# A hybrid S5 / SSD / gated-DeltaNet trunk: side tasks cut into smaller pieces, the residual's scale and bias applied in the output projection, and two merge gates computed earlier

## Chip, cores and metric

One Trainium2 chip, one of its cores. The metric is the device time of one execution in microseconds (us), the median of several runs; lower is better.

## What is computed

Two decoder layers (DEPTH = 2) over 528 tokens (16 meta tokens and 512 of input), width 1024, everything in float32. An input LayerNorm makes `h`; each layer then does

```python
proj = h @ w_in[layer]
y_a = _s5_branch(...)      # diagonal complex state space, 48 groups, then gelu and a half-GLU
y_b = _ssd_branch(...)     # Mamba-2 style chunked scan, SiLU gate, RMSNorm
y_c = _gdn_branch(...)     # gated DeltaNet, 6 heads, chunked, RMSNorm, SiLU gate
branches = jnp.stack([y_a, y_b, y_c], axis=2)
outs = jnp.einsum('btnw,nwd->btnd', branches, w_branch[layer])
gates = jax.nn.sigmoid(gate_logits.reshape(bsz, t, N_BRANCH, D_MODEL) + b_gate[layer])
merged = jnp.sum(gates * outs, axis=2)
h = _layer_norm(ALPHA * h + merged @ w_out[layer], ln_g[layer], ln_b[layer])
```

and the meta tokens are dropped at the end. `_layer_norm` is `(z - mean) * rsqrt(var + eps) * g + b`.

## The kernel before

**Main stream and tasks.** The kernel writes its instructions in one pass of a Python program, and each engine runs its own instructions in the order in which they were written. The main stream is a list of items (`layer_items`, line 1704). Most are `Gemm` (line 570): 128 output channels over all tokens, the weights in pairs of 128x128 tiles, one pair being a "sub". For each sub ScalarE rounds the raw weight `wr` to `wh`, and VectorE (sometimes GpSimd) makes the rest `wl = wr - wh` (`Sub.prep`, line 509); TensorE then multiplies `wh` by the high part of the activations, `wh` by their low part, and `wl` by their high part: 12 matmuls of 264 columns for a sub. At most four subs are prepared ahead (`NSUB`), and four raw weight loads of two subs each (`NRAW`).

Everything else (convolution tails, the scalars of the heads, the gated-DeltaNet, SSD and S5 branches, norms) is a task: a Python generator that gives way at each `yield`. After each step of a Gemm, `pump` (line 458) lets tasks run that are due by a clock that the program keeps of its own writing. A plain `yield` makes a task due when what it just wrote is thought to end, `yield LEAD` 1.5 us before that. All that a task writes between two yields stands in one run in the queues of its engines, and the next split `wl` stands behind it.

**Names that matter here.** `head_scalars` (line 691) makes per-head scalars on tiles `sc`, `sc_p`, `sc_g`; `conv` (665) adds three taps to a channel tile (`q`, `k`, `v`, `x` or `bc` from `craw`); `rsqrt` (363) is eleven short VectorE instructions; `s5_params` (1268) makes the S5 tables on `s5t`, `s5f` through `together` (1256), which gave way after ten steps. `s5_task` (1545) runs one half of the S5 groups: `s5_mats` makes `Z`, `T` and `V` for four groups (T goes through DRAM: three writes `dK<-Kt`, eight reads `s5t<-dK`), `s5_core` multiplies `V` with the input `ub` (eight loads `ub<-dus`), scans, and multiplies again into `Y`, which ScalarE copies to `ys`. When a half is done, `ys` goes to DRAM (`dys<-ys`), and `s5_gelu` reads it back as `yc` and makes the rows `vhi`, `vlo` that the GLU's Gemms read. The loads all stand in one queue, that of SyncE (SP), in the order in which they were written.

**The layer's end.** In `merge_all` (1815) each branch n and each eighth d of the width has a gate Gemm and an output Gemm. Some gates (`KEPT`, line 52) are computed early, at places where the main stream has no other work, written to DRAM (`dgate`) and read back (`Back`) when they are due. The order is: branch 2, four kept gates, branch 1, wait for task `v` (the gelu rows), six GLU Gemms, six `za` Gemms, branch 0, and `OutProj` (1883) in four quarters of 256 columns, chunk of tokens by chunk.

**The residual.** LayerNorm leaves `z` normalised but without `g` and `b` (those reach the transposed `hTh`, `hTl` in `to_channels`, 393). A task `keep_task` (1686), due when all five token tiles are normalised, multiplies each by `g` and adds `b` with two instructions of 1024 columns (`ln_affine`, 388) and writes the tile to `hdram`, from where `o_pre` (1871) loads it as `zt` for the output projection.

Of the kernel before, what the change touches and what calls it, by code (L numbers as in the profile page):

```python
# [17 lines left out]
P = 128  # L18
D = 1024
# [32 lines left out]
KEPT = [(0, d) for d in range(2, 8)] + [(1, 6), (1, 7)]  # L52
# [187 lines left out]
def hybrid_trunk(ctx: ExitStack, tc: tile.TileContext, A: dict, out: bass.AP):  # L240
# [122 lines left out]
    def rsqrt(dst, x, shape, tag):  # L363
# [23 lines left out]

    def ln_affine(z, n, gb, bb):
        tte(z[:n], z[:n], gb[:n], MUL)
        yield LEAD  # L390
        tte(z[:n], z[:n], bb[:n], ADD)
# [273 lines left out]
    def conv(l, ci, ps, dst, bias):  # L665
# [8 lines left out]
        yield  # L674
# [16 lines left out]
    def head_scalars(l, smT, hs):  # L691
# [23 lines left out]
        V.reciprocal(out=s, in_=s)  # L715
        tt(V, s, s, e, MUL)
# [95 lines left out]
    def gdn_task(l, grp, hs, st):  # L812
# [26 lines left out]
        rsqrt(r, x, sh, "g_r")  # L839
# [256 lines left out]
        rsqrt(f, m, h3, "go_f")  # L1096
# [123 lines left out]
    def ssd_post(l, hs, st, to):  # L1220
# [12 lines left out]
        rsqrt(r, m, [P, NC], "sn_r")  # L1233
# [22 lines left out]
    def together(*chains):  # L1256

        chains, n = list(chains), 0
        while chains:
# [4 lines left out]
            if n >= 10:  # L1264
# [3 lines left out]
    def s5_params(l):  # L1268
# [124 lines left out]
        for k in (1, 2, 4):  # L1393
# [4 lines left out]
            tt(V, t[1], xi, yi, MUL)  # L1398
            tt(V, t[2], xr, yi, MUL)
# [56 lines left out]
    def s5_mats(l, hf, qd, q, b, out):  # L1456
# [88 lines left out]
    def s5_task(l, hf, st):  # L1545
# [3 lines left out]
        nxt = {}  # L1549
        yield from s5_mats(l, hf, 0, s5q, w["b"], nxt)  # L1550
# [120 lines left out]

    class Do:
# [7 lines left out]
    def ln_task(l, z, t0, n, st):  # L1680

        yield from ln_norm(z, n, st)
        yield
        yield from to_channels(z, t0, n, l)

    def keep_task(l, zs, gb, bb):

        for z, t0, n in zs:
            yield from ln_affine(z, n, gb, bb)
            yield  # L1690
            DMA.dma_start(out=hdram[l][t0:t0 + n, :], in_=z[:n])
# [471 lines left out]
```

## Time and profile before

| what | value |
|---|---|
| median of 3 runs (lowest to highest) | 1737.22 us (1730.16 to 1737.72) |
| the profiled execution, its own time | 1739.94 us |
| its span, first to last instruction | 1738.2 us |
| mean granted clock of TensorE | 0.972 of full speed |
| TensorE (PE) matmuls, busy | 1627.3 us, 94% |
| VectorE (DVE), busy | 1317.2 us, 76% |
| ScalarE (ACT), busy | 824.4 us, 47% |
| GpSimd (POOL), busy | 173.4 us, 10% |

In the rows below, a group of instructions reads `out<-in` by the program's names, with the shape, the number of them and their time. `[7.06 <-DVE wl]` is idle time of the engine ahead of the instruction and what ended it. Nearly all instructions carry line 229, a helper's, so names tell them apart. `PEclk` is the clock granted to TensorE as a share of full speed.

### The profile page before, as it was taken

To read this page: it belongs to the slowest core of one execution; us is meant where nothing else is said; L and a number is where in the kernel's file an instruction comes from. 1 tells how busy PE (TensorE), PEld (TensorE's weight loads), DVE (VectorE), ACT (ScalarE), POOL (GpSimd) and SP (SyncE) were. 2 spreads that over 40 slices of the span, in tenths; PEclk is the share of its full clock that TensorE was granted. 3 is DMA by queue.
4 is the path that set the end of the run, shared out by engine and by line. 5 is a ranking of instruction groups with operands and counts; after the bars stand their busy time and mean duration, and the time that the engine had idled before them with its cause. 6 is when DMAs were issued, how large, how long until landed. Compare 5 with 4: busy or idle time off the path is not lost.

```text
span 1738.2 us, 40832 instructions
## 1 busy us (share of the span) xinstructions
PE 1627.3 (94%) x15583; PEld 1554.7 (89%) x15583; DVE 1317.2 (76%) x3399; ACT 824.4 (47%) x2059; POOL 173.4 (10%) x314
## 2 busy tenths in 40 slices
PE   6799899989999899999989998999899989999997
PEld 5789899988899899999979998898888988999997
DVE  7987869778967876685678687697799869765665
ACT  5356554335673334434254655453366533453432
POOL 5000000110001000100130000101100001000013
PEclk9899999989999999999999999999999999999998
DMA  5223321343234444334423233223431452533352
GB/s 162 92 80 84 97 69 56 102 75 88 58 76 113 91 120 129 97 94 136 138 75 117 81 94 90 56 62 92 87 89 51 105 106 84 140 121 113 115 186 82
DMA packets 160147, 169.71 MB, mean 98 GB/s; under 512 B 67344, under 2 KB 98192, under 8 KB 159952
## 3 DMA queue, kind: packets, MB, share of 16 engines
q1 hardware_dynamic: 159952, 167.10, 34.8%
q8 instruction: 123, 2.02, 0.5%
q14 instruction: 72, 0.59, 0.1%
HBM read 144.40 MB, written 22.64 MB: 96 GB/s over the span
## 4 chain that ended last, share of the span: by engine, by line
PE 68%; DVE 16%; DMA 6%; issue 3%; ACT 3%; SPq 2%; POOL 1%; DVEq 0%; POOLq 0%; ACTq 0%
PE pj L229 49%; PE wo L229 5%; DVE wl L229 3%; SPq L229 2%; DMA wr<-in_w_main_dram 2%; PE y L229 2%; PE Y L229 2%; DMA dU<-UL 1%; PE seg L229 1%; DVE s5t L229 1%; DVE pr L229 1%; DVE s5w L229 1%; PE o L229 1%; PE z L229 1%; DVE UL L229 1%
## 5 line engine op out<-in xcount | busy, mean ns | idle before, releaser
L229 PE MATMUL pj<-hTh,wl 128*128 128x264 f32 (+1 forms) x2432 | 504.0, 288 | 35.1 <-DVE wl L229 34.9
L229 PE MATMUL pj<-hTh,wh 128*128 128x264 f32 (+1 forms) x2432 | 525.8, 297 | 1.5 <-ACT wh L229 1.5
L229 PE MATMUL pj<-hTl,wh 128*128 128x264 f32 (+1 forms) x2432 | 502.5, 287 | 0.0
L229 ACT ACTIVATE wh<-wr 128x256 fp32r<-128x256 f32 x820 | 327.2, 413 | 275.1 <-PE pj L229 227.7
L229 DVE TENSOR_TENSOR wl<-wr,wh 128x256 fp32r<-128x256 f32 x743 | 301.2, 429 | 163.6 <-ACT wh L229 160.8
L229 PEld LDWEIGHTS pj<-hTh,wl 128*128 128x128 f32 x2432 | 385.0, 193 | 41.0 <-DVE wl L229 40.7
L229 PEld LDWEIGHTS pj<-hTh,wh 128*128 128x128 f32 x2432 | 383.2, 193 | 9.5 <-issue 4.3
L229 PEld LDWEIGHTS pj<-hTl,wh 128*128 128x128 f32 x2432 | 385.8, 192 | 0.0
L229 POOL TENSOR_TENSOR wl<-wr,wh 128x256 fp32r<-128x256 f32 x77 | 64.9, 843 | 908.0 <-ACT wh L229 847.5
L229 PE MATMUL pj<-yhi,wh 128*128 128x264 f32 (+1 forms) x576 | 118.0, 286 | 2.0 <-ACT yhi L229 1.0
L229 PE MATMUL pj<-ylo,wh 128*128 128x264 f32 (+1 forms) x576 | 116.0, 283 | 0.5 <-DVE ylo L229 0.5
L229 PE MATMUL pj<-yhi,wl 128*128 128x264 f32 (+1 forms) x576 | 115.8, 282 | 0.0
L229 PEld LDWEIGHTS pj<-yhi,wh 128*128 128x128 f32 x576 | 88.5, 188 | 3.7 <-ACT yhi L229 1.4
L229 PEld LDWEIGHTS pj<-ylo,wh 128*128 128x128 f32 x576 | 88.6, 188 | 0.9 <-DVE ylo L229 0.9
L229 PEld LDWEIGHTS pj<-yhi,wl 128*128 128x128 f32 x576 | 88.7, 188 | 0.2 <-DVE wl L229 0.2
L229 ACT ACTIVATE segr<-triu,sc_glo 128x128 fp32r<-128x128 f32 (+1 forms) x168 | 52.3, 375 | 1.0 <-PE sS L229 1.0
L229 ACT ACTIVATE segr<-triu,sc_ghi 128x128 fp32r<-128x128 f32 (+1 forms) x168 | 52.3, 375 | 0.4 <-DVE x L229 0.2
L229 ACT ACTIVATE craw<-pj 128x528 f32<-128x528 f32 x56 | 34.0, 608 | 37.6 <-PE pj L229 37.5
L229 PE MATMUL wo<-wo,mhi 128*128 128x256 f32 x256 | 47.4, 283 | 0.2 <-DVE zt L229 0.2
L229 ACT ACTIVATE gth<-pj,pars 128x528 f32<-128x528 f32 (+1 forms) x48 | 33.1, 690 | 29.3 <-PE pj L229 29.3
L229 DVE TENSOR_TENSOR s5w<-s5w,s5w 128x132 f32<-128x132 f32 (+1 forms) x144 | 40.8, 297 | 3.0
L229 DVE TENSOR_TENSOR s5w<-V,tab 128x264 f32<-128x264 f32 x48 | 18.5, 427 | 32.2 <-PE V L229 32.2
(387 smaller groups left out, 2801.7 us busy)
## 6 DMA issues: line engine op xcount, KB each, us to landing
wr<-in_w_main_dram SPq DMA_DIRECT2D x304, 256.0 KB
wr<-in_w_branch_dram SPq DMA_DIRECT2D x48, 256.0 KB
wr<-in_w_out_dram SPq DMA_DIRECT2D x32, 256.0 KB
s5t<-dK SPq DMA_DIRECT2D x192, 32.0 KB
wr<-in_w_branch_dram SPq DMA_DIRECT2D x48, 128.0 KB
zt<-hdram SPq DMA_DIRECT2D x8, 512.0 KB
dus<-us SPq DMA_DIRECT2D x12, 264.0 KB
ub<-dus SPq DMA_DIRECT2D x32, 99.0 KB
```

Source lines behind the costliest of these rows:

```text
L229: r = f(*args, **kw)
```

## The change

It has four parts.

1. **Smaller pieces.** `yield LEAD` is added inside `rsqrt` (after each of three rounds), between the taps of `conv`, in `head_scalars`, in the S5 mats and tables; `together` gives way after six steps in place of ten; `s5_task` gives way after every part of a core or of the mats, where it ran one part of each.
2. **`ub` first.** `s5_task` writes the eight `ub` loads ahead of the first `s5_mats`, where they stood behind it.
3. **Residual.** `keep_task` and `ln_affine` go. The normalised tile is written to `hdram` at once, ahead of the transposes, and `OutProj` multiplies by `g` and adds `b` on each chunk's 256 columns ahead of the chunk's products. `g` and `b` of a layer are loaded with the first two `zt` tiles, into slots of the tag `bc`.
4. **Gates, and what the SSD norm waits for.** The last two kept gates are (0, 0) and (0, 1) in place of (1, 6) and (1, 7). So branch 1 computes its gates 6 and 7 in place, ahead of the wait for `v`, and branch 0 reads all eight back. `ssd_post` waits for the mark `xc` (branch 2 merged) where it waited for the second S5 half `fB`.

```diff
-KEPT = [(0, d) for d in range(2, 8)] + [(1, 6), (1, 7)]
+KEPT = [(0, d) for d in range(2, 8)] + [(0, 0), (0, 1)]
...
             stt(dst, t, 1.5, dst, ADD, MUL)
+            yield LEAD
...
         for i in range(3):
             fma(dst, raw[:, i:i + T], w[:, i:i + 1], dst)
-        yield
+            yield LEAD if i < 2 else None
...
         V.reciprocal(out=s, in_=s)
+        yield LEAD
...
             stt(p, p, 1.0 / d, s2, ADD, MUL)
+            if d in (13, 7):
+                yield LEAD
         stt(p, p, 1.0, s, ADD, MUL)
+        yield LEAD
...
-        while f"fB{l}" not in done:
+        while f"xc{l}" not in done:
             yield WAIT
...
-            if n >= 10:
+            if n >= 6:
...
         tte(z, bc(b["c"][:, gl], 2, 9), bc(q["pr"][:, gg], 3, 16), MUL)
+        yield LEAD
         tte(u, bc(b["cx"][:, gl], 2, 9), bc(q["pi"][:, gg], 3, 16), MUL)
+        yield LEAD
...
-        nxt = {}
-        yield from s5_mats(l, hf, 0, s5q, w["b"], nxt)
         while "us" not in st:
             yield WAIT
...
             DMA.dma_start(out=ub[16 * j:16 * j + 16], in_=src[:, :, NB8 * j:NB8 * j + NB8])
+        nxt = {}
+        yield from s5_mats(l, hf, 0, s5q, w["b"], nxt)
...
-                    if next(t, "end") == "end":
+                    r = next(t, "end")
+                    if r == "end":
                         live.remove(t)
-                if live:
-                    yield
+                    else:
+                        yield r
...
         yield from ln_norm(z, n, st)
         yield
+        keep(l, z, t0, n)
         yield from to_channels(z, t0, n, l)
-    def keep_task(l, zs, gb, bb):
...
+    def keep(l, z, t0, n):
+        DMA.dma_start(out=hdram[l][t0:t0 + n, :], in_=z[:n])
...
+                    zh = zt[c][:n, 256 * qn:256 * qn + 256]
+                    for x, op in zip(zt["in"], (MUL, ADD)):
+                        tte(zh, zh, x[:n, 256 * qn:256 * qn + 256], op)
                     if n < 32:
                         few_products(c)
```

**VectorE, layer 0, the head scalars beside the first convolutions.** `sc` and `sc_p` belong to `head_scalars`, `q` to a convolution, `s5t` to the S5 tables, `wl` are the weight splits that TensorE needs. Before:

```order
75 L229 TENSOR_SCALAR sc_576<-sc_576 128x90
76 L229 RECIPROCAL sc_576<-sc_576 128x90
77 L229 TENSOR_TENSOR sc_576<-sc_576 128x90 x2
78 L229 TENSOR_SCALAR sc_p_658<-sc_576 128x90
79 L229 SCALAR_TENSOR_TENSOR sc_p_658<-sc_p_658,sc_576 128x90 x8
80 L229 TENSOR_SCALAR sc_576<-sc_576 128x90
81 L229 SCALAR_TENSOR_TENSOR sc_576<-sc_p_658,sc_576 128x90
82 L229 TENSOR_TENSOR sc_g_670<-sc_576,pars 128x90
83 L229 TENSOR_SCALAR sc_g_670<-sc_g_670,m_107 128x18
84 L229 CAST sc_ghi_673<-sc_g_670 128x90
85 L229 SCALAR_TENSOR_TENSOR q_588<-craw_589,pars,q_588 128x528 x3
86 L229 TENSOR_TENSOR wl_685<-wr_502,wh_684 128x256
```

Now:

```order
65 L229 SCALAR_TENSOR_TENSOR q_578<-craw_579,pars,q_578 128x528
66 L229 TENSOR_TENSOR sc_566<-sc_566 128x90 x2
67 L229 TENSOR_SCALAR sc_p_625<-sc_566 128x90
68 L229 SCALAR_TENSOR_TENSOR sc_p_625<-sc_p_625,sc_566 128x90 x2
69 L229 TENSOR_TENSOR wl_636<-wr_444,wh_635 128x256
70 L229 SCALAR_TENSOR_TENSOR s5t_513<-s5t_513 128x48 x6
71 L229 SCALAR_TENSOR_TENSOR q_578<-craw_579,pars,q_578 128x528
72 L229 TENSOR_TENSOR wl_661<-wr_495,wh_660 128x256
73 L229 SCALAR_TENSOR_TENSOR sc_p_625<-sc_p_625,sc_566 128x90 x3
74 L229 TENSOR_TENSOR wl_685<-wr_495,wh_684 128x256
```

Between two splits there stood 21 instructions of the scalars and the convolution; now three splits stand among them.

**SyncE's queue, layer 0, the start of the second S5 half.** `wr` are raw weights, `dK` and `s5t` the way of T through DRAM, `ub` the S5 input. Before:

```order
204 L229 DMA dK<-Kt_8068 16x128
205 L229 DMA dK<-Kt_8068 32x128
206 L229 DMA dK<-Kt_8068 16x128
207 L229 DMA s5t_8076<-dK 16x4x128 x8
208 L229 DMA wr_8095<-in_w_main_dram 128x512
209 L229 DMA wr_8141<-in_w_main_dram 128x512
210 L229 DMA ub_8155<-dus_4413 16x24x66 x8
```

Now:

```order
202 L229 DMA ub_8111<-dus_4394 16x24x66 x8
203 L229 DMA wr_8134<-in_w_main_dram 128x512
204 L229 DMA wr_8174<-in_w_main_dram 128x512
205 L229 DMA wr_8213<-in_w_main_dram 128x512
206 L229 DMA dK<-Kt_8232 16x128
207 L229 DMA dK<-Kt_8232 32x128
208 L229 DMA dK<-Kt_8232 16x128
209 L229 DMA s5t_8240<-dK 16x4x128 x8
```

The eight `ub` loads now stand ahead of the eleven transfers of T, and T's come last.

**SyncE's queue, layer 1, the end of the second S5 half.** `dys` is the S5 output on its way to DRAM, `yc` its way back, `dgate` a kept gate. Before:

```order
599 L229 DMA dys_21715<-ys_20412 16x24x66 x8
600 L229 DMA dgate_88<-gth_21730 128x512
601 L229 DMA wr_21738<-in_w_main_dram 128x512
602 L229 DMA wr_21775<-in_w_branch_dram 128x512
603 L229 DMA dgate_88<-gth_21808 128x512
604 L229 DMA wr_21816<-in_w_branch_dram 128x256
605 L229 DMA wr_21855<-in_w_main_dram 128x512
606 L229 DMA wr_21895<-in_w_main_dram 128x512
607 L229 DMA wr_21932<-in_w_branch_dram 128x512
608 L229 DMA wr_21950<-in_w_branch_dram 128x256
609 L229 DMA yc_21961<-dys_19584 128x3x528
```

Now:

```order
610 L229 DMA dys_22179<-ys_20668 16x24x66 x8
611 L229 DMA yc_22189<-dys_19897 128x3x528
612 L229 DMA wr_22203<-in_w_branch_dram 128x512
613 L229 DMA wr_22221<-in_w_branch_dram 128x256
614 L229 DMA wr_22258<-in_w_main_dram 128x512
```

The read back of the first half now stands directly behind the writes of the second.

## Rows read from the trace of the kernel before

**Rows 1.** Page, part 1: busy time, share of the span, instructions.

```profile
PE 1627.3 (94%) x15583; PEld 1554.7 (89%) x15583; DVE 1317.2 (76%) x3399; ACT 824.4 (47%) x2059; POOL 173.4 (10%) x314
```

**Rows 2.** Chain that ended last, its longest piece: start, length, instructions.

```profile
759.90 77.15 PE pj L229 x632
```

**Rows 3.** Waits of PE: who for whom, us in total, times, longest.

```profile
PE pj L229 <- DVE wl L229: 35.4, 27, 7.1
PE V L229 <- DMA wr<-in_w_main_dram: 11.2, 3, 3.9
...
PE fb L229 <- DVE q L229: 3.0, 1, 3.0
...
PE V L229 <- DMA ub<-dus: 2.0, 1, 2.0
```

**Rows 4.** Timeline near 60 us, DVE and PE: start, length, instruction, idle before.

```profile
59.20 2.27 DVE L229 SCALAR_TENSOR_TENSOR sc_p<-sc_p,sc 128x90 f32<-128x90 f32 x8
...
62.58 2.37 DVE L229 SCALAR_TENSOR_TENSOR q<-craw,pars,q 128x528 f32<-128x528 f32 x3
...
65.34 0.81 PE L229 MATMUL pj<-hTh,wl 128*128 128x264 f32 x2 [7.06 <-DVE wl L229]
```

**Rows 5.** Stretches of 20 us: busy PE, PEld, DVE, ACT, POOL; granted clock; DMA; GB/s.

```profile
60.00:80.00 20.00, 14.66 (x92) 14.30 (x93) 19.27 (x75) 6.28 (x16) 0.20 (x2) 0.74 0.14 44
400.00:420.00 20.00, 17.85 (x166) 15.58 (x166) 14.35 (x50) 10.24 (x38) 1.20 (x1) 0.83 0.29 87
...
860.00:880.00 20.00, 20.00 (x177) 19.24 (x177) 12.65 (x33) 5.60 (x16) 2.98 (x4) 1.00 0.25 83
...
920.00:940.00 20.00, 16.56 (x112) 15.99 (x111) 17.32 (x44) 7.02 (x20) 0.20 (x2) 0.83 0.36 117
1240.00:1260.00 20.00, 15.28 (x185) 14.32 (x184) 12.17 (x45) 6.12 (x14) 2.05 (x5) 0.83 0.44 92
```

**Rows 6.** Tile `xin`, layer 0's residual: ns of one (min/median/max), first and last start.

```profile
L229 DVE TENSOR_TENSOR xin<-xin,ln_in_g x5: 1205/1214/1881, 32.4 to 55.0; 128x1024 f32<-128x1024 f32 x4, 16x1024 f32<-16x1024 f32 x1
```

**Rows 7.** The loads of `ub`: SyncE's timeline, and a piece of the chain.

```profile
557.36 1.94 SPq L229 DMA_DIRECT2D s5t<-dK  x1
...
560.29 4.15 SPq L229 DMA_DIRECT2D ub<-dus  x8
...
371.65 7.24 DMA ub<-dus
```

**Rows 8.** Groups of instructions by form: busy us, ns of one, idle before.

```profile
L229 DVE TENSOR_TENSOR wl<-wr,wh 128x256 fp32r<-128x256 f32 x743 | 301.2, 429 | 163.6 <-ACT wh L229 160.8 <-PE pj L229 1.0
...
L229 DVE BATCH_NORM_STATS2 lnst<-zt 128x6 f32<-128x256 f32 x32 | 13.7, 428 | 1.1
L229 DVE SCALAR_TENSOR_TENSOR zt<-zt,wo 128x256 f32<-128x256 f32 x32 | 13.4, 417 | 22.7 <-PE wo L229 20.5 <-DMA zt<-hdram 2.1
...
L229 POOL TENSOR_TENSOR wl<-wr,wh 128x256 fp32r<-128x256 f32 x77 | 64.9, 843 | 908.0 <-ACT wh L229 847.5 <-DMA dys<-ys 19.9 <-DVE vlo L229 19.8
```

**Rows 9.** Timeline near 39 us: a POOL instruction and a split on DVE beside it.

```profile
39.15 3.92 POOL L229 TENSOR_SCALAR_AFFINE_SELECT sel<-ones 18x768 bf16<-18x768 bf16 x3
39.40 1.11 DVE L229 TENSOR_TENSOR wl<-wr,wh 128x256 fp32r<-128x256 f32 x1
```

**Rows 10.** Timeline at the end of the second S5 half, layer 0, then layer 1.

```profile
649.04 0.39 ACT L229 ACTIVATE ys<-Y 128x264 f32<-128x264 f32 x1 [1.56 <-PE Y L229]
...
666.31 0.65 ACT L229 ACTIVATE gl<-yc 128x528 f32<-128x528 f32 x1 [1.10 <-DMA yc<-dys]
...
1498.84 0.39 ACT L229 ACTIVATE ys<-Y 128x264 f32<-128x264 f32 x1 [2.32 <-PE Y L229]
...
1524.00 0.65 ACT L229 ACTIVATE gl<-yc 128x528 f32<-128x528 f32 x1 [3.31 <-DMA wr<-in_w_main_dram]
...
1566.21 0.71 DVE L229 TENSOR_TENSOR vlo<-yc,vhi 128x528 fp32r<-128x528 f32 x1 [0.71 <-ACT vhi L229]
```

**Rows 11.** The six `vlo` rows of layer 0, as Rows 6.

```profile
L229 DVE TENSOR_TENSOR vlo<-yc,vhi x6: 709/709/710, 671.3 to 710.9; 128x528 fp32r<-128x528 f32 x6
```

More of the change, by code (lines that the diff above doesn't have):

```diff
@@ L386, in ln_norm @@
             act(z[:n, c], z[:n, c], AF.Identity, bias=ve[:n, 1:2], scale=rs[:n])
[L388 to L391, printed above, removed]
     def to_channels(h, t0, n, l):
@@ L838, in gdn_task @@
         r = small(sh, "g_r")
-        rsqrt(r, x, sh, "g_r")
+        yield from rsqrt(r, x, sh, "g_r")
         ts(V, r, r, 0.5, MUL)
@@ L1095, in gdn_task @@
         f = small(h3, "go_f")
-        rsqrt(f, m, h3, "go_f")
+        yield from rsqrt(f, m, h3, "go_f")
         tt(V, f, f, cq, MUL)
@@ L1232, in ssd_post @@
         r = small([P, NC], "sn_r")
-        rsqrt(r, m, [P, NC], "sn_r")
+        yield from rsqrt(r, m, [P, NC], "sn_r")
         yield from put_rows(hs, "rn", r.unsqueeze(2), 1, "rowk", 3)
-        while f"fB{l}" not in done:
+        while f"xc{l}" not in done:
             yield WAIT
@@ L1463, in s5_mats @@
         tte(z, bc(b["c"][:, gl], 2, 9), bc(q["pr"][:, gg], 3, 16), MUL)
+        yield LEAD
         tte(u, bc(b["cx"][:, gl], 2, 9), bc(q["pi"][:, gg], 3, 16), MUL)
+        yield LEAD
         tte(z, z, u, SUB)
@@ L1485, in s5_mats @@
         clock.end = 0.0
+        yield LEAD
         v = small([P, 4, P], "s5v")
@@ L1489, in s5_mats @@
         tte(v4, bc(b["y"][:, gl], 2, 8), bc(q["pr"][:, gg, 1:9], 3, 16), MUL)
+        yield LEAD
         tte(u, bc(b["yx"][:, gl], 2, 8), bc(q["pi"][:, gg, 1:9], 3, 16), MUL)
+        yield LEAD
         tte(v4, v4, u, ADD)
@@ L1670, in run, with __init__ @@
             finish(*self.names)
+    class Mark:
+        def __init__(self, name):
+            self.name = name
+        def run(self):
+            done.add(self.name)
     class Do:
@@ L1683, in ln_task @@
         yield
+        keep(l, z, t0, n)
         yield from to_channels(z, t0, n, l)
-    def keep_task(l, zs, gb, bb):
[L1688 to L1691, printed above, removed]
-            yield LEAD
+    def keep(l, z, t0, n):
+        DMA.dma_start(out=hdram[l][t0:t0 + n, :], in_=z[:n])
     def last_task(z, t0, n, st, gb, bb):
@@ L1876, in o_pre @@
                 zt["st", c] = small([P, 4, 6], "lnst", bufs=5)
-            if 0 not in which:
+            if 0 in which:
+                zt["in"] = [row_vec(A["ln_in" + k] if l == 0 else A["ln" + k][l - 1:l, :],
+                                    flat(sp.tile([P, 2, T], F32, tag="bc", name=nm("res"), bufs=2))[:, 0:D])
+                            for k in ("_g", "_b")]
+            elif lastl:
                 zt["gb"], zt["bb"] = (row_vec(A[k][l:l + 1, :], tok_tile(k)) for k in ("ln_g", "ln_b"))
@@ L1945, in run @@
                         products(c, range(KD - 1 if qn == 0 and c < 2 else 0, KD))
-                    zh = zt[c][:n, 256 * qn:256 * qn + 256]
                     stt(zh, zh, ALPHA, ps[c][:n], MUL, ADD)
@@ L2011, in layer_items @@
         merge_all(2, xc, 6, 8)
+        items.append(Mark("xc" + L))
         def f_v():
@@ L2037, in layer_items @@
             items.append(Need(*[f"ln{DEPTH}{c}" for c in cs]))
-        else:
-            items.append(Start(f"keep{l + 1}", lambda: keep_task(l + 1, [(zt[c], *cs[c]) for c in cs], zt["gb"], zt["bb"]),
-                               *[f"ln{l + 1}{c}" for c in cs]))
         return items
@@ L2052, in hybrid_trunk @@
     DMA.dma_start(out=dKz[:, :, 128:240], in_=bc(zpad, 1, 12))
-    gb, bb = (row_vec(A[k], nu(k)) for k in ("ln_in_g", "ln_in_b"))
     lnst = [small([P, 4, 6], "lnst", bufs=5) for _ in ROWT]
@@ L2062, in ln_in @@
         yield
+        keep(0, z, t0, n)
         yield from to_channels(z, t0, n, 0)
@@ L2076, in hybrid_trunk @@
         start(f"ln0{c}", lambda: first[c])
-    start("keep0", lambda: keep_task(0, [(z, *r) for z, r in zip(xin, ROWT)], gb, bb),
-          [f"ln0{c}" for c in range(len(ROWT))])
     for it in items:
```

## The prediction

> **What bounds the kernel now.** I read the busy times first. PE (TensorE) is busy 94% of the span, DVE (VectorE) 76%, nothing else over half [rows 1]. So PE bounds it, and what can be won is PE's idle time, 1738.2 - 1627.3 = 111 us, and the time in which its clock is low. Its full pace is in the longest piece of the chain: 632 matmuls in 77.15 us, 0.122 us each [rows 2]. A sub (12 matmuls) is 1.46 us of PE work, and the four subs that may be prepared ahead are 5.9 us.
>
> The waits of PE come next [rows 3]. Two kinds stand out. 27 waits for the split `wl` make 35.4 us. Four waits of the matmul `V`, which needs the `ub` loads, make 11.2 + 2.0 = 13.2 us: three are put down to a weight load, but `V` reads no weights, and its other input is `ub`. The rest of the 111 us is mostly the first 20 us, the layer boundary and the tail, which the change hardly touches.
>
> The longest `wl` wait, 7.06 us, shows the mechanism [rows 4]. From 58 us DVE does head scalars (eight `sc_p` alone take 2.27 us), then three convolution taps (2.37 us), and only then the split that PE needs. Both are tasks, each written in one run; the run adds up to 7.9 us by the durations of its forms, longer than the 5.9 us that the prepared subs cover at best.
>
> Last, the clock. After these waits it drops to half (1.2 of 2.4 GHz) for a few us. Four such stretches of 20 us, among the deepest, read 0.74 once and 0.83 three times [rows 5]: 0.26 x 20 + 3 x 0.17 x 20 = 15.4 us at full speed lost. PE was busy 64.4 of these 80 us, so about 12.4 us of it was paid in work.
>
> **The sum, part by part**, against the profiled execution's own 1739.9 us.
>
> *Smaller pieces.* The total work is the same, only its order differs, so the saving is in the runs between splits. I added up, for each run of DVE instructions between two splits in either order, the trace's mean duration of each form. Before, 41 runs are over 5 us with 84 us above that mark; now 17 with 47 us. Without the four runs at the start and the layer boundary, where PE waits for the norm anyway, it is 55 and 27 us: half. At the place of the 7.06 us wait the longest run falls from 7.9 to 4.9 us. Ends: 0 (each wait returns at the next split) and -35.4 us. Halving gives -18; the longest wait goes nearly whole, and two long runs remain (10.0 and 13.9 us, in the gated DeltaNet). I take -21, nearer to the halving than to either end. Part of it is the residual's doing: ten instructions of 1.2 us [rows 6] leave DVE's fullest stretch, 19.27 of 20 us busy at 60 to 80 us [rows 5]. On their own they cost only what they add to a run, so they are in the -21.
>
> *`ub` first.* Before, `ub`'s issue stood behind T's three writes and eight reads, which wait for each other; the last read takes 1.94 us to issue, `ub`'s eight 4.15 us, and the last load lands 7.24 us after its issue begins [rows 7]. From issue to landing is about 10.5 us. Now Z, K and V of the first mats lie between `ub` and its use, and by the order 66 to 132 main matmuls stand there, 8 to 16 us at 0.122 us, with other matmuls besides. So most of the 13.2 us is covered. What is late next is T, whose eleven transfers now come last: from K to Y only 72 to 126 main matmuls are left, where 138 to 222 were. I take -10 (ends 0 and -13.2).
>
> *The clock.* Where the idle goes, so does the low clock behind it. Of the 12.4 us I take three quarters, -9 (ends 0 and about -20, as the shallower dips, which I didn't add up, may go too).
>
> *One wait of `fb` for `q`*, 3.0 us [rows 3], stands in a DVE run of 12.1 us that is cut to 4.3: -2 (0 to -3).
>
> *Residual in the output projection.* 72 instructions of 256 columns are new, 26 on DVE and 46 on POOL by the order. The nearest rows are 417 ns on DVE and 843 ns on POOL [rows 8]. They stand ahead of a chunk's products, which are 24 matmuls, about 2.9 us of PE. For a chunk DVE has 417 + 428 ns today and its share of splits; POOL has two instructions, 1.7 us. Both fit under PE, which is the cover. In the first quarter the multiply needs `zt`, where only the later add needed it, and DVE already waited 2.1 us for it once [rows 8]. I take +2 (ends 0 and +18; the upper end is that every POOL instruction stops DVE, worked out among the rivals).
>
> What speaks for the upper end is a row: while POOL ran, a split took 1.11 us on DVE where the group's mean is 0.43 [rows 8, 9], so the two do get in each other's way. The Trainium skill (SBUF — State Buffer, "SBUF: two separate sides") says that GpSimd and a VectorE instruction with two SBUF inputs take one pair of ports in turns, each for its whole length; the row agrees, and it speaks against putting 46 instructions on GpSimd beside VectorE's splits. By that rule in full the POOL rival below would hold, 1718 us; by the rows of one chunk alone, +2 and the 1702 us of the forecast.
>
> *Gates.* Two gate Gemms a layer (96 matmuls, 11.7 us) move from behind `za` to ahead of the wait for `v`. Work neither grows nor shrinks. At branch 0's start the cover is gone: the last `za` row needs five steps on ScalarE and DVE of some 0.7 us, as a `vlo` row takes [rows 11], 3.5 us, and branch 0's first Gemm has 30 matmuls (3.7 us) that don't need it. +1 (0 to +7).
>
> *The S5 half's end.* Finer turns make the S5 chain longer: its last Y comes 222 main matmuls later in layer 0, 282 in layer 1, and from there to the GLU 438 are left, where 564 and 624 were. Also `yc` follows `dys` directly. ScalarE's first `gl` stands in its queue and waited 1.10 and 3.31 us for its data [rows 10], with 8 and 16 splits of weights between `ys` and `gl`; now 6. A ScalarE that waits there holds back `wh`. The SSD norm no longer waits for `fB`, which spreads its rows. +4 (0 to +24, below).
>
> Sum: -21 - 10 - 9 - 2 + 2 + 1 + 4 = -35, so 1705 us. The profiled execution (1739.9) is 2.7 us above the runs' median (1737.2), so I say 1702.
>
> **Rivals.**
>
> *Half the gain is eaten by the next waits* (S5 late). From the last `ys` to the end of the last `vlo` took 649.0 to 711.6 = 63 us in layer 0 and 1498.8 to 1566.9 = 68 us in layer 1 [rows 10, 11]. The new order leaves 438 x 0.122 = 53 us. If the chain keeps its length, PE stands 10 and 15 us at the GLU or ahead of it: +24 in place of +4, so 1702 + 20 = 1722. For it: the rows of `vhi` now end one and seven subs ahead of the GLU in ScalarE's order, not eleven and more. Against: much of those 63 us is the program's own spacing, and `vlo` alone needs about 5.5 us a row.
>
> *POOL stops DVE in the output projection.* 40 full-width POOL instructions and six of 16 rows at 843 ns are 39 us; with DVE's own 26 x 0.417 = 11 us, over two stretches of 44 us in which DVE is 63% busy today (56 us, from the stretch at 860 us) [rows 5], DVE would need 106 of 88 us: +18 in place of +2, so 1718 if all of it is exclusive. Against: half of DVE's work there reads PSUM or has a single input.
>
> *It does not do what it says.* The runs are cut, but PE meets each wait one split later, and T's wait replaces `ub`'s: 1733 to 1740. For it: 777 splits now stand among nearly the same sum of DVE work. Against: the count of long runs, which halves.
>
> *Slower.* The place is the wait for `v`. Its chain goes through SyncE's queue, where `yc` waits for `dys` to land with the weight loads behind it. PE is one to one with any delay beyond 53 us. Without its +4 the sum is -39, so the sign turns where the chain takes 53 + 20 = 73 us in each layer, 5 and 10 us longer than before. At 80 us, as when the two reads of `yc` each wait 6 to 8 us more, the idle is 2 x 27 = 54 us: 1737 - 39 + 54 = 1752. Against: nothing in the new order makes these transfers larger, and `yc` stands ahead of more weight loads than it did.
>
> **How the numbers follow.** The forecast (a gain of 22 to 60 us) 0.64, S5 late 0.13, POOL 0.08, no effect 0.09, slower 0.06. The range goes down to 1678, where `wl` waits fall by 30, `ub` by 13 and the clock by 20, and up to 1727, which takes in the two partial cases. A measurement can tell about 0.5% (8.7 us) from no change. Below 1728.5: the forecast, the two partial cases, 0.84; within: 0.10; above 1746: 0.06.
>
> **What would show it.** Right: PE's waits for `wl` at 10 to 18 us in total, none over 4 us; `V` waiting under 4 us in all; granted clock 0.98 or more; no `keep` work on DVE at 40 to 80 us. Wrong: `wl` waits still at 30 us; a new wait of `Y` for `s5t` or of `pj<-vhi` for `vlo`; PE below 95% of its pace in the output projection, with DVE near full there.

## The result: 23 us faster, for other reasons than those of the sum

The changed kernel takes 1714.37 us (median of 4 runs, 1712.81 to 1716.22); the kernel before, run beside it, 1737.47 (1730.16 to 1738.61). The ratio is 0.9865 with a 95% interval of 0.983 to 0.9899. A second timing on another chip gave 0.9866 (0.9837 to 0.9895). The forecast was 1702, so 12 us of the 35 are missing. The kernel before had medians of 1737 to 1746 us on the chips used, so below the runs are compared by their ratios to it.

The page of the changed kernel, part 1, answers to [rows 1]:

```profile
PE 1619.9 (95%) x15583; PEld 1546.9 (90%) x15583; DVE 1302.4 (76%) x3413; ACT 821.2 (48%) x2057; POOL 196.4 (11%) x352
```

PE's idle time is 1711.5 - 1619.9 = 92 us, where it was 111, and POOL has 38 instructions and 23 us more. The waits of PE, as in [rows 3] (who for whom, us in total, times, longest):

```profile
PE pj L229 <- DVE wl L229: 16.2, 16, 2.4
...
PE pj L229 <- ACT wh L229: 7.6, 5, 3.0
PE wo L229 <- DVE wl L229: 6.2, 11, 1.9
PE pj L229 <- DVE gth L229: 4.7, 2, 2.4
...
PE wo L229 <- DVE wo L229: 1.9, 5, 0.9
```

The waits for `wl` halved as forecast (35.4 to 16.2, none over 2.4). Those of `V`, 13.2 us, are not in the list any more. Three kinds are new or larger: the output projection waits for its splits (6.2 + 1.9), branch 0 waits for gates that are read back (4.7), and 5.6 of the 7.6 us for `wh` are two places where ScalarE stood for `yc`. One row of each of the last two, from the timeline (start, length, instruction, idle before):

```profile
662.65 0.64 ACT L229 ACTIVATE gl<-yc 128x528 f32<-128x528 f32 x1 [5.39 <-DMA yc<-dys]
...
784.45 0.48 PE L229 MATMUL pj<-yhi,wh 128*128 128x264 f32 x2 [2.34 <-DVE gth L229]
```

Three of the stretches of [rows 5] again, at the same times (busy PE, PEld, DVE, ACT, POOL; granted clock; DMA; GB/s):

```profile
60.00:80.00 20.00, 17.12 (x132) 16.00 (x131) 15.98 (x61) 7.93 (x22) 0.57 (x3) 1.00 0.19 58
400.00:420.00 20.00, 19.77 (x176) 17.77 (x176) 18.21 (x46) 15.27 (x46) 1.14 (x1) 1.00 0.21 58
1240.00:1260.00 20.00, 20.00 (x208) 17.92 (x207) 17.04 (x39) 16.59 (x53) 1.17 (x1) 1.00 0.25 71
```

The clock is whole in all three, and DVE has 15.98 us of work at 60 to 80 us where it had 19.27.

The place of the gain and of the loss is seen best when the span is cut at five points of each layer: the first sum of branch 2 (`acc<-gth,pj`), of branch 1 (`acc<-acc,gth`), the first output product of branch 0, the first and the last `wo` product. The us between them, from the timelines (layer 0 / layer 1; the first row counts from the span's start or the last `wo` of layer 0):

| stretch | before | change | residual as before | pieces alone | pieces and ub | ub alone | parts that paid |
|---|---|---|---|---|---|---|---|
| to branch 2 | 478.5 / 453.9 | 453.5 / 431.2 | 475.0 / 425.5 | 477.1 / 436.3 | 471.1 / 430.4 | 480.9 / 446.7 | 458.1 / 419.7 |
| branch 2 to 1 | 195.8 / 180.2 | 182.8 / 171.2 | 179.4 / 172.8 | 218.1 / 201.4 | 201.4 / 193.4 | 180.4 / 172.2 | 183.1 / 187.8 |
| branch 1 to 0 | 127.6 / 120.2 | 136.5 / 127.7 | 137.8 / 129.8 | 128.5 / 117.8 | 126.7 / 119.0 | 128.4 / 118.8 | 130.1 / 117.6 |
| to output projection | 35.0 / 33.9 | 37.9 / 37.1 | 35.4 / 34.3 | 35.1 / 33.9 | 35.1 / 33.8 | 35.0 / 33.9 | 35.2 / 33.9 |
| output projection | 54.8 / 45.7 | 65.0 / 53.9 | 54.4 / 46.2 | 54.5 / 46.4 | 54.9 / 45.8 | 54.5 / 46.4 | 60.5 / 46.0 |
| ratio to before | 1 | 0.9865 | 0.9778 | 1.0104 | 0.9907 | 0.9809 | 0.9684 |

The change won 25 + 23 us ahead of branch 2 and 13 + 9 between branches 2 and 1, and gave back 10 + 8 in the output projections, 9 + 7.5 between branches 1 and 0 and 3 + 3 ahead of the output projection. Rows two and three also trade work: between branches 2 and 1 PE runs 1709 and 1701 matmuls in the change, where it ran 1824 and 1749, and between branches 1 and 0 1105 and 1064, where it ran 993 and 999. So part of those gains and losses is the same work in another row. The runs below say which part did what.

### The profile page after: what moved, and what is told of

Its sections match the earlier page's. It is cut to its first block, busy times and chain, and to the rows that moved or that the text cites. A ratio compares the mean times of both kernels' runs of the same rounds, so it can differ in the third digit from the quotient of the medians.

```text
span 1711.5 us, 40925 instructions
## 1 busy us (share of the span) xinstructions
PE 1619.9 (95%) x15583; PEld 1546.9 (90%) x15583; DVE 1302.4 (76%) x3413; ACT 821.2 (48%) x2057; POOL 196.4 (11%) x352
## 3 DMA queue, kind: packets, MB, share of 16 engines
q1 hardware_dynamic: 159952, 167.10, 35.1%
## 4 chain that ended last, share of the span: by engine, by line
PE 72%; DVE 15%; DMA 6%; issue 3%; ACT 2%; SPq 2%; POOL 0%; DVEq 0%; POOLq 0%; ACTq 0%
PE pj L229 52%; PE wo L229 4%; DVE wl L229 3%; PE y L229 2%; SPq L229 2%; DMA dU<-UL 2%; PE Y L229 2%; PE seg L229 1%; PE o L229 1%; DVE s5t L229 1%; DMA gth<-dgate 1%; DVE pr L229 1%; DVE zt L229 1%; DMA yc<-dys 1%; PE z L229 1%
## 5 line engine op out<-in xcount | busy, mean ns | idle before, releaser
L229 PE MATMUL pj<-hTh,wl 128*128 128x264 f32 (+1 forms) x2432 | 498.6, 285 | 11.4 <-DVE wl L229 11.1
L229 DVE TENSOR_TENSOR wl<-wr,wh 128x256 fp32r<-128x256 f32 x749 | 315.1, 435 | 168.1 <-ACT wh L229 161.5
L229 PEld LDWEIGHTS pj<-hTh,wl 128*128 128x128 f32 x2432 | 380.5, 190 | 15.7 <-DVE wl L229 15.4
L229 PEld LDWEIGHTS pj<-hTh,wh 128*128 128x128 f32 x2432 | 379.0, 191 | 9.4 <-issue 3.5
L229 PE MATMUL pj<-yhi,wh 128*128 128x264 f32 (+1 forms) x576 | 120.2, 290 | 11.9 <-ACT wh L229 5.6
L229 PEld LDWEIGHTS pj<-yhi,wh 128*128 128x128 f32 x576 | 90.0, 192 | 14.4 <-issue 6.0
L229 PE MATMUL wo<-wo,mhi 128*128 128x256 f32 x256 | 51.8, 298 | 2.4 <-DVE wo L229 1.9
L229 PEld LDWEIGHTS wo<-wo,mhi 128*128 128x128 f32 x256 | 42.2, 201 | 4.9 <-DVE wo L229 2.9
```

What stands on the lines that cost most here:

```text
L229: r = f(*args, **kw)
```

## Experiments

"Ratio" is the time over that of the kernel before on the same chip, with its 95% interval.

**1. The third part undone.**

```diff
-                    for x, op in zip(zt["in"], (MUL, ADD)):
-                        tte(zh, zh, x[:n, 256 * qn:256 * qn + 256], op)
...
+            items.append(Start(f"keep{l + 1}", lambda: keep_task(l + 1, [(zt[c], *cs[c]) for c in cs], zt["gb"], zt["bb"]),
```

> The changed kernel with its third part undone: the task that scales and shifts the residual is back behind the norm, and the output projection has no multiply and no add. Theory A (the 72 new instructions in the output projection, mostly GpSimd's, lengthen VectorE's splits beside them and cost about 18 us over the two output projections, which grew by 10.2 and 8.2 us): both output projections return to about 55 and 46 us from the first residual product to the last, and 5 to 12 us come back where the task stands in VectorE's fullest stretches at the start of the layers, so 1701 to 1709. Rival B (the output projection grew because the loads of its weights stand behind the loads of the residual, its scale and its bias, or for another reason than the instructions; the residual's part is a gain at the start of the layers): 1717 to 1726, with output projections still near 65 and 54 us or only part of the way back.

Measured: 1705.7 us, ratio 0.9778 (0.972 to 0.9836). Theory A: the output projections are back at 54.4 and 46.2 us. But the first stretch of layer 0 is 14 to 22 us longer than in the profiles with the residual moved (453.5 to 461.1), and that of layer 1 no longer at all. So the third part gains in layer 0's front and costs in both output projections; as a whole it made the kernel slower (0.9778 against 0.9865, whose intervals just touch; experiments 9 and 11, which differ in the residual alone, layer 0's on VectorE and layer 1's back in the task, stand clear of each other at 0.9833 and 0.972).

**2. The first part alone.**

```diff
             stt(dst, t, 1.5, dst, ADD, MUL)
+            yield LEAD
...
-                if live:
-                    yield
+                    else:
+                        yield r
```

> The kernel before with the first part of the change alone: the added places to give way; the residual, the loads of ub and the gates stand as before. Theory A (the cut runs of VectorE return most of the wait for the splits wl, and the clock behind it): PE's waits for wl fall from 35 to 12 to 18 us, the four waits of V for ub stay near 13 us, output projections as before, 1700 to 1712. Rival C (the cuts alone do little, and the front of each layer gained from the residual's ten and ten instructions leaving VectorE and from ub): wl waits stay above 25 us, 1722 to 1735.

Measured: 1762.51 us, ratio 1.0104 (1.0049 to 1.0159): slower. Neither theory had this. The `wl` waits fell as theory A said; others grew. PE's waits:

```profile
PE pj L229 <- DVE wl L229: 18.9, 18, 3.3
PE Y L229 <- DMA s5t<-dK: 10.6, 3, 4.2
...
PE VT L229 <- DVE s5v L229: 8.2, 5, 2.7
PE V L229 <- DMA wr<-in_w_main_dram: 7.2, 2, 3.8
```

Most of the loss stands between branches 2 and 1 (+22 and +21 us). The timeline there shows the last two rounds of layer 0's second S5 half, T's read (`s5t`), `Y`, the transpose of the next V (`VT`), one behind the other, and the first matmul of the main stream behind them:

```profile
652.87 4.56 SPq L229 DMA_DIRECT2D s5t<-dK  x8
...
658.96 0.49 PE L229 MATMUL Y<-ub,s5t 128*64 128x66 f32 x4 [4.15 <-DMA s5t<-dK]
...
664.88 1.08 PE L229 MATMUL VT<-ident,s5v 128*128 128x128 f32 x4 [2.69 <-DVE s5v L229]
...
670.59 0.49 PE L229 MATMUL Y<-ub,s5t 128*64 128x66 f32 x4 [2.79 <-DMA s5t<-dK]
...
676.13 0.81 PE L229 MATMUL pj<-yhi,wh 128*128 128x264 f32 x2 [2.16 <-ACT yhi L229]
```

In these 23 us PE has only the S5's own small matmuls and two of the SSD norm's; the main stream (`pj`) goes on when the half is done. The last 16 us of it and the 4 us behind, in numbers:

```profile
660.00:680.00 20.00, 11.23 (x100) 8.19 (x98) 10.53 (x25) 3.99 (x9) 0.00 (x0) 0.50 0.27 46
```

The clock is at its lower level for all of it. PE's order says why: the last `Y` of the first half stands behind 2592 main matmuls, where it stood behind 2346. Of these 246, 102 are there when the first of its six rounds ends (2022 for 1920); the next two rounds then take 132 and 156 main matmuls, for 96 each before. The second half starts later too (its `ub` loads at 585.5 us for 560.3), and the main stream, at its wait for the SSD norm, which waits for that half, has nothing to give.

**3. The same, with the SSD norm waiting for the mark.**

```diff
-        while f"fB{l}" not in done:
+        while f"xc{l}" not in done:
```

> The kernel with the pieces alone, and in addition the SSD norm waiting for the mark of branch 2 in place of the second S5 half; gates, ub and residual as in the kernel before. Theory F (in the kernel with the pieces alone the S5 halves ended about 22 us later, and TensorE stood still because the SSD norm, and with it branch 1, waited for the second half): branch 1's first sum comes 180 to 200 us after branch 2's first, where it was 218 and 201; part of the lateness comes back at the wait for v ahead of the GLU; 1722 to 1742 in all. Rival G (the S5 chain itself is what TensorE waits for, through T, V and ub; who waits for its end decides nothing): 1752 to 1765, with the waits of Y for s5t and of VT for s5v still near 19 us.

Measured: 1762.93 us, ratio 1.0096 (1.0064 to 1.0129). Theory F is right about the place and wrong about the sum: branch 1's first sum comes 188.6 and 171.7 us after branch 2's, but branch 1 to 0 takes 156 and 148 us, 28 more than in the kernel before. The whole lateness reappears at the GLU:

```profile
PE pj L229 <- ACT vhi L229: 21.9, 6, 9.3
PE pj L229 <- DVE wl L229: 19.3, 22, 2.7
```

This is what the prediction's rival "S5 late" describes: the half ends late, and PE stands at the GLU.

**4. `ub` first alone.**

```diff
-        nxt = {}
-        yield from s5_mats(l, hf, 0, s5q, w["b"], nxt)
         while "us" not in st:
...
             DMA.dma_start(out=ub[16 * j:16 * j + 16], in_=src[:, :, NB8 * j:NB8 * j + NB8])
+        nxt = {}
+        yield from s5_mats(l, hf, 0, s5q, w["b"], nxt)
```

> The kernel before with the second part of the change alone: the eight loads of ub ahead of the first mats of a half. Theory D (each part helps by itself): V's waits fall from 13.2 us to under 4, and the time is 8 to 15 us under the kernel before. Rival E (the loads of T now come last, and Y waits for s5t in place of V for ub; the part pays only with the others): within 5 us of the kernel before, with a wait of Y for s5t that was not there.

Measured: 1710.62 us, ratio 0.9809 (0.977 to 0.9848): 33 us, more than the whole change, though the intervals overlap (0.9848 and 0.983). Theory D is right in kind and far too small; there is no new wait for `s5t` over 0.2 us. PE's waits; then the stretch in which `V` had waited 3.7 us (its clock was 0.91); then the stretch behind the place where `V` had waited 2.0 us, in the kernel before and now:

```profile
PE pj L229 <- DVE wl L229: 37.2, 26, 7.1
...
PE V L229 <- DMA wr<-in_w_main_dram: 2.3, 1, 2.3
```

```profile
560.00:580.00 20.00, 19.44 (x233) 18.62 (x232) 19.65 (x45) 8.27 (x21) 3.34 (x4) 1.00 0.35 88
```

```profile
380.00:400.00 20.00, 20.00 (x273) 18.92 (x269) 14.32 (x42) 6.40 (x15) 1.34 (x3) 0.83 0.29 78
```

```profile
380.00:400.00 20.00, 20.00 (x297) 18.88 (x296) 18.65 (x56) 9.48 (x24) 2.86 (x5) 1.00 0.42 107
```

The span is 28.3 us shorter than the profiled one before. PE's idle time fell by 14.4 us (110.9 to 96.5), 10.9 of it in `V`'s waits; PE's busy time fell by 13.9 us with the same 15583 matmuls, most of it the clock: a mean of 0.978 for 0.972 is 1738.2 x 0.028 - 1709.9 x 0.022 = 11 us at full speed. That sets two chips side by side; the runs of the kernel before on this chip have a median clock of 0.968 and a median span of 1742.8 us, these 0.978 and 1708.9, so here the clock is 18 of 34 us. The `wl` waits did not change. And the S5 halves come earlier: in layer 0 the second one's `ub` loads are issued at 537.8 us, where it was 560.3, and the last `Y` of the two halves stands behind 72 and 90 main matmuls fewer.

**5. The cuts without those in the S5 rounds.** Experiment 2, but `s5_mats` and the loop over rounds as before.

```diff
-                    r = next(t, "end")
-                    if r == "end":
+                    if next(t, "end") == "end":
                         live.remove(t)
-                    else:
-                        yield r
+                if live:
+                    yield
```

> The kernel with the pieces alone, but the rounds of the S5 halves (their mats and cores) give way as in the kernel before; the cuts in the convolution, the head scalars, the short rsqrt and the S5 tables stay. Theory J (the finer turns in the rounds are what makes the halves end late): the first half's writes dys begin near 491 us and the second's near 650 us as in the kernel before (532 and 674 with all pieces), the waits for wl stay at 17 to 22 us, V's waits at 13 us, and the time is 0.7 to 1.5% under the kernel before, 1719 to 1733 against 1745. Rival K (every cut in any task pushes the S5 halves back in the program's order, since tasks take turns by one clock): the halves still end over 10 us late, TensorE waits for Y, VT and V over 25 us, 1745 to 1762.

Measured: 1722.04 us, ratio 0.9881 (0.9858 to 0.9904), 2.2% under experiment 2: theory J for the time. PE's waits:

```profile
PE pj L229 <- DVE wl L229: 15.7, 17, 3.4
PE V L229 <- DMA wr<-in_w_main_dram: 14.9, 4, 4.4
...
PE y L229 <- DVE go_ft L229: 2.3, 1, 2.3
```

Rival K has a share: the first half's `dys` begins at 506 us, between 491 and 532, and the second's at 656 (2424 and 3354 main matmuls ahead of the last `Y`). The 102 main matmuls by which the first round ends later are here too (2022), so they come from the cuts outside the rounds.

Here the `wl` waits are at their new value, `V`'s at their old one, and the mean clock is 0.971, as before. Beside the runs of the kernel before on this chip (medians of 0.969 and 1740.1 us, here 0.9705 and 1720.3) the clock is 3 of 20 us. But this is a difference of gains and losses. At 920 us, where the kernel before read 0.83 [rows 5], it is now whole; at 320 us, behind the wait of `y` for `go_ft`, which the kernel before doesn't have, it is low for the whole stretch. The kernel before at 320 us, then this run:

```profile
320.00:340.00 20.00, 20.00 (x260) 18.43 (x257) 13.36 (x43) 6.98 (x18) 4.17 (x8) 1.00 0.37 121
```

```profile
320.00:340.00 20.00, 20.00 (x197) 18.27 (x194) 5.69 (x16) 5.63 (x14) 2.73 (x5) 0.51 0.36 117
...
920.00:940.00 20.00, 19.82 (x161) 19.44 (x160) 18.71 (x44) 8.96 (x22) 0.47 (x2) 1.00 0.50 162
```

That stretch alone costs 0.49 x 20 = 9.8 us at full speed. In experiments 1 and 2 the same wait is 2.4 and 2.3 us long, and the stretch reads 0.84 and 0.85.

**6. Pieces and `ub` first together.** The edits of experiments 2 and 4.

```diff
+                    else:
+                        yield r
...
+        nxt = {}
+        yield from s5_mats(l, hf, 0, s5q, w["b"], nxt)
```

> The first and second part of the change together: all pieces, and ub first; residual, gates and the mark as in the kernel before. Theory L (ub first also brings each half's rounds forward, so that the pieces no longer end them late): V, Y and VT wait under 8 us in all, wl 17 to 20 us, ratio 0.974 to 0.981 to the kernel before, that is 1700 to 1712 against 1745, and gates and mark add nothing. Rival M (the halves still end later than before and the SSD norm waits for the second one; only the mark and the moved gates let both be had): branch 1's first sum comes over 190 us after branch 2's first in layer 0, 1722 to 1750.

Measured: 1725.74 us, ratio 0.9907 (0.9882 to 0.9931), branch 2 to 1 in 201.4 us: rival M. `Y` again waits for T:

```profile
PE pj L229 <- DVE wl L229: 18.4, 17, 3.4
...
PE Y L229 <- DMA s5t<-dK: 8.2, 2, 4.2
```

With `ub` first, the pieces still cost 1% (0.9907 against 0.9809). From here to experiment 1 the gates and the mark are added, and the ratio falls to 0.9778. Between branches 2 and 1 that saves 22.0 and 20.6 us, between 1 and 0 it costs 11.1 and 10.8, where the last S5 rounds now lie. So the fourth part pays for the first. How is argued from the program's order and not shown: the mark lets branch 1 go on, and the two moved gates put 96 more matmuls between the last `Y` and the GLU. All three together (0.9778) can't be told from `ub` first alone (0.9809): the intervals overlap.

**7. The residual on VectorE alone.**

```diff
-                        tte(zh, zh, x[:n, 256 * qn:256 * qn + 256], op)
+                        tt(V, zh, zh, x[:n, 256 * qn:256 * qn + 256], op)
```

> The changed kernel with all multiplies and adds of the residual in the output projection on VectorE, none on GpSimd. Theory A in its form 'GpSimd's instruction holds up VectorE's splits': the splits wl and wo in the output projection fall from 610 to 730 ns back to about 430 each, both output projections shrink by 4 to 7 us, 1701 to 1707. Rival A2 (VectorE's capacity is what ran out, whoever does the residual): the splits are short again, but VectorE has 46 more instructions of 0.42 us, 19 us, and the output projections stay at 65 and 54 us or longer: 1712 to 1722. Rival B (weight loads behind the residual's loads): within 3 us of 1714.

**8. The residual's scale and bias left out.**

```diff
-                    for x, op in zip(zt["in"], (MUL, ADD)):
-                        tte(zh, zh, x[:n, 256 * qn:256 * qn + 256], op)
```

> The changed kernel without the multiply by the norm's scale and the add of its bias on the residual: that part of the computation is left out, the loads of scale and bias stay. Theory A (the instructions cost, not the loads): the whole 18 us return, the splits are at about 430 ns, 1694 to 1699. Rival B (the loads cost): 1709 to 1715, output projections near 65 and 54 us.

Measured: on VectorE 1707.08 us, ratio 0.9787 (0.9738 to 0.9837); left out 1697.25 us, 0.9718 (0.9663 to 0.9773). The output projections take 60.7 and 48.2 us on VectorE, 54.0 and 45.6 left out. So the loads of scale and bias cost nothing there (rival B is out), and 19.3 us is the price of the 72 instructions as the change places them, 9.3 us that of the same 72 on VectorE, each from one profile (experiment 10's would make the first 22.8). Rival A2 is out too: VectorE has 46 instructions more, and both output projections are shorter. Layer 0's output projection in the changed kernel, groups by form (busy us, ns of one, idle before), and its stretch, first in the kernel before and then now:

```profile
L229 POOL TENSOR_TENSOR zt<-zt,res 128x256 f32<-128x256 f32 x23 | 18.0, 795 | 0.8
L229 DVE TENSOR_TENSOR wl<-wr,wh 128x256 fp32r<-128x256 f32 x13 | 9.1, 735 | 0.0
L229 DVE TENSOR_TENSOR wo<-wr,wo 128x256 fp32r<-128x256 f32 x10 | 7.0, 730 | 2.7 <-ACT wo L229 2.7
L229 DVE BATCH_NORM_STATS2 lnst<-zt 128x6 f32<-128x256 f32 x15 | 6.4, 428 | 0.5
L229 DVE SCALAR_TENSOR_TENSOR zt<-zt,wo 128x256 f32<-128x256 f32 x15 | 6.2, 416 | 9.5 <-PE wo L229 9.3
...
L229 POOL TENSOR_TENSOR zt<-zt,res 16x256 f32<-16x256 f32 x6 | 4.9, 811 | 0.2
```

```profile
837.00:892.00 55.00, 52.92 (x468) 49.14 (x466) 37.33 (x97) 18.45 (x46) 9.68 (x13) 1.00 0.36 111
```

```profile
811.00:876.00 65.00, 57.38 (x465) 51.95 (x465) 48.80 (x109) 18.79 (x46) 30.12 (x39) 0.95 0.29 94
```

The same with the residual on VectorE:

```profile
L229 DVE TENSOR_TENSOR zt<-zt,res 128x256 f32<-128x256 f32 x30 | 12.5, 415 | 0.5
...
L229 DVE TENSOR_TENSOR wl<-wr,wh 128x256 fp32r<-128x256 f32 x14 | 5.8, 446 | 0.0
...
L229 DVE TENSOR_TENSOR wo<-wr,wo 128x256 fp32r<-128x256 f32 x12 | 4.5, 419 | 0.0
```

```profile
816.00:878.00 62.00, 55.27 (x472) 49.85 (x471) 52.94 (x138) 18.93 (x47) 6.66 (x10) 1.00 0.31 102
```

With POOL at work for 30 us, a split takes 730 ns in the mean; with POOL at 6.7 us, 419 to 446. The instructions with one input from SBUF (`lnst`) or one from PSUM (`zt<-zt,wo`) keep their 428 and 416 ns. That is theory A in the form named for experiment 7. The Trainium skill (SBUF — State Buffer, "SBUF: two separate sides") says of just these, a VectorE instruction with two SBUF inputs and a GpSimd instruction that reads SBUF, that whichever starts first holds the ports they share for its whole length and the other waits. The rows agree in which instructions are slowed; the mean split pays 300 ns of a POOL instruction's 795. Of the 10 us by which the stretch grew, PE's idle time is 5.5 (7.6 for 2.1), and the clock, 0.95 for 1.00, 3. The timeline of the changed kernel shows how it reaches PE:

```profile
841.11 7.65 POOL L229 TENSOR_TENSOR zt<-zt,res 128x256 f32<-128x256 f32 x9
...
842.94 2.71 DVE L229 TENSOR_TENSOR wl<-wr,wh 128x256 fp32r<-128x256 f32 x3
...
847.24 0.94 DVE L229 TENSOR_TENSOR wl<-wr,wh 128x256 fp32r<-128x256 f32 x1
848.24 0.58 PE L229 MATMUL wo<-wl,mhi 128*128 128x256 f32 x1 [1.92 <-DVE wl L229]
```

The program sends nearly two of three of these instructions to POOL because its own clock expects GpSimd to be done first; that choice is what lengthens VectorE's splits.

**9. Two queue orders.** The first two gates of branch 0 are read back ahead of the residual's loads, and the gelu starts later after `yc` is asked for.

```diff
-        items.append(Do(lambda: o_pre((0, 1))))
-        merge_all(0, xa, 0, 8)
+        merge_all(0, xa, 0, 8, late=lambda: o_pre((0, 1)))
...
-        yield
+        for _ in range(5):
+            yield WAIT
```

> The changed kernel with two queue orders changed: the first two read-backs of gates of branch 0 stand ahead of the loads of the residual (two zt tiles, scale and bias), and the gelu of an S5 half starts 7.5 us of program time after the load of yc is issued, where it started at the next turn. Theory H (both losses are queues): TensorE's waits for gth at branch 0 (4.7 us) go, the step from branch 0's start to the output projection falls from 37.9 and 37.1 us to 35 and 34; the waits for wh behind yc (5.6 us) go; the output projections stay at 65 and 54 us; 6 to 12 us under the changed kernel, so 1702 to 1708. Rival I (the later gelu makes the wait for v longer, or the residual's loads then come late for the output projection): within 3 us of 1714, with a new wait ahead of the GLU or of zt.

Measured: 1717.45 us, ratio 0.9833 (0.9803 to 0.9863), which overlaps the change's own, so no gain is shown. The wait for `gth` is gone and that stretch takes 35.5 and 34.6 us, as theory H says. The other half is rival I: waits for `vhi` of 2.6 us appear, layer 1 takes 133.3 us between branches 1 and 0, for 127.7, and the wait of ScalarE only changed its name, from `yc` to a weight load behind it in SyncE's queue:

```profile
1504.77 0.42 ACT L229 ACTIVATE wh<-wr 128x256 fp32r<-128x256 f32 x1 [7.34 <-DMA wr<-in_w_branch_dram]
```

So ScalarE's order was not the cause there; the load behind `dys` and `yc` comes as late as `yc` does.

**10. The change again.** The changed kernel, with no edit.

> The changed kernel itself, so that it stands on the same chip and beside the same runs of the kernel before as the runs of this call: 1710 to 1720 by every theory, ratio 0.982 to 0.988.

Measured: 1718.22 us, ratio 0.9866, with output projections of 69.0 and 53.4 us.

**11. Layer 0's residual in its output projection, on VectorE; layer 1's by the task.** With the two orders of experiment 9.

```diff
+                    if l == 0:
+                        for x, op in zip(zt["in"], (MUL, ADD)):
+                            tt(V, zh, zh, x[:n, 256 * qn:256 * qn + 256], op)
```

> A version put together from what the first four runs showed: layer 0's residual in the output projection, all on VectorE (the front of layer 0 was 14 to 21 us shorter without the task, the output projection 6 us longer on VectorE, 11 with GpSimd); layer 1's residual by the task behind the norm, as in the kernel before (it cost nothing there); and the two queue orders of the run above. If the parts add up: 1705 (residual as before) less 14, plus 6, less 5 to 10 for the queues: 1688 to 1696. If the front of layer 0 gains nothing that lasts: 1700 to 1708.

Measured: 1697.3 us, ratio 0.972 (0.9684 to 0.9756), just above the range for "the parts add up". It beats the change.

**12. The parts that paid.** The kernel before with `ub` first, the cuts of experiment 5 and the residual of experiment 11; gates, mark and S5 rounds as before.

```diff
         nxt = {}
         yield from s5_mats(l, hf, 0, s5q, w["b"], nxt)
...
+                    if l == 0:
+                        for x, op in zip(zt["in"], (MUL, ADD)):
+                            tt(V, zh, zh, x[:n, 256 * qn:256 * qn + 256], op)
```

> The kernel before with the parts that paid in the runs so far, and none of the others: ub first; the pieces without the finer turns in the S5 rounds; layer 0's residual in the output projection on VectorE alone; layer 1's residual, the gates and the SSD norm's wait as in the kernel before. If the S5 rounds end no later than in the kernel before, the gains stand side by side: ub first 0.981, less about 0.010 for the cut runs (wl waits at 15 to 18 us), less 0.004 for layer 0's residual (14 us won at the front, 6 to 8 lost in its output projection): 0.960 to 0.970, 1674 to 1690 against 1742. If instead the gains of ub and of the pieces are the same idle time won twice, or the gates and the mark are needed: 0.974 to 0.982, 1698 to 1712.

Measured: 1689.15 us (median of 6), ratio 0.9684 (0.9654 to 0.9713): the gains stand side by side, and this version beats both kernels. PE's waits for `wl`:

```profile
PE pj L229 <- DVE wl L229: 12.8, 15, 3.4
```

The product of experiments 4 and 5 is 0.9809 x 0.9881 = 0.969, so layer 0's residual adds nothing that these intervals show; its front is 20 us shorter than before and its output projection 6 longer, while branch 2 to 1 of layer 1 stays 8 us longer than before. It isn't idle time (PE stands 5.9 us there, where it stood 7.5); the cause stays open.

## Why the prediction was right, and where it was not

The sign, the range and three of the signs named were right: `wl` at 16.2 us (10 to 18 named), no wait of `V`, a clock of 0.980 (0.976 and 0.977 in two of the four runs). That the sum of -35 came near -23 is luck. Added one after the other, `ub` first gives -33 us (experiment 4), the pieces on top of it +17 (6), gates and mark -22 (1) and the residual +15 (the change), from the ratios, each step uncertain by 7 to 12 us. The gain as a whole rests on `ub` first, which the sum had at -10 and its share of the clock; the sum's largest term, the pieces, is a loss at that place, and large errors of both signs met.

- *Smaller pieces, -21.* The term itself holds: `wl` waits fell by 19.2 us, and the cuts outside the S5 rounds alone gave 1.2%, 21 us. What failed is the step "the total work is the same, only its order differs, so the saving is in the runs between splits". The order also sets when an S5 half ends. The prediction had counted it (222 and 282 main matmuls later) and put +4 on it. Alone the pieces made the kernel 1% slower.
- *`ub` first, -10.* Mis-sized: it measured -33 us alone. The 13.2 us of waits went as said. The clock adds 11 us in the profiles, 18 by the runs on one chip; what the earlier S5 halves add was not separated.
- *The clock, -9.* About right for the change: beside the kernel before on one chip (experiment 10, medians of 0.975 and 0.969) it is 11 us. What it comes from differs: experiment 4 gains the clock with no gain in `wl`, and in experiment 5 what rose behind `wl` waits was lost behind other waits. The step "where the idle goes, so does the low clock behind it" left out that a new order makes new waits, with a low clock behind them.
- *`fb` for `q`, -2.* That row is gone, but not by the cut run alone: it is gone in experiment 4 too, which cuts nothing.
- *Residual, +2.* Mis-sized: the output projections grew by 10.2 + 8.2 us. The step that failed is "both fit under PE, which is the cover": it gave each instruction its own length and left out the 300 ns that a split takes longer beside POOL's instructions, so that PE waits for splits (6.2 + 1.9 us) and its clock falls (0.95). The rows of the POOL rival [rows 8, 9] had said so. That the sum of this rival, +18, meets 18.4 is chance: it has VectorE run out of time, 106 of 88 us, in two stretches of 44 us, and they take 54.8 and 45.7 us. The sign named for it came half true: PE was busy 57.38 of 65 us there, 88%, with VectorE at 75% and not near full. The part's gain, 14 to 22 us in layer 0's front, had no term of its own: the prediction counted it among the pieces.
- *Gates, +1.* 2.3 us of waiting at branch 0 in each layer; within its range of 0 to 7. The cause is not the chain of the last `za` row, as said, but the read-back standing behind the residual's loads (experiment 9).
- *The S5 half's end, +4.* No wait for `vhi` came. ScalarE stood 5.4 and 5.5 us for `yc`, 5.6 us of PE. But the term's small size hangs on the fourth part, which the prediction priced as a side matter: without mark and moved gates, the same pieces and `ub` take 1.3% more time (experiment 6 against 1).

Left open: how much of the fourth part is the mark and how much the two gates, with `ub` first (no run had one of them alone there).

## What to carry to other kernels

A task that gives way more often ends later; before cutting it, find who waits for its end, and cut those whose end nobody waits for. Price a wait of TensorE by its length and the clock behind it, look for the waits that a new order makes, and test each part of a change alone, since a large gain can pay for a loss beside it. When work may go to GpSimd, count what it adds to each VectorE instruction with two SBUF inputs that runs at the same time, not only its own length.

## What the runs showed of the hardware that was not expected

A VectorE split of 256 columns went from 419 or 446 ns to 730 or 735 ns while GpSimd ran back to back, and the instructions with one SBUF input kept their 428 and 416 ns. GpSimd's instruction on 16 partitions took 811 ns, no less than the 795 ns of one on 128. And a wait of TensorE of 2.3 or 2.4 us (`y` for `go_ft`) was followed by 20 us at a mean clock of 0.51 in one run (experiment 5) and of 0.84 and 0.85 in two others (1 and 2), with PE busy all of the 20 us in each; so what one wait costs in clock can't be read from its length alone.
